# Four shifted taps in 32-column groups on TensorE: a depthwise convolution and its projection recast

## The chip, the cores and the metric

The kernel runs on one core of a Trainium2 chip. Its time is device microseconds from the first to the last instruction of one execution, median of several; lower is better. The engines are TensorE (PE, with its weight loads PEld), VectorE (DVE), ScalarE (ACT), GpSimd (POOL) and SyncE (SP, which here only issues DMAs).

## The reference

A decoder trunk of two layers on 512 tokens of 1024 channels, in float32. The change lies in the first half of the first layer, the Conformer convolution module; the rest is named only.

```python
def conformer_conv(x, w_pw1, b_pw1, w_dw, b_dw, ln_g, ln_b, w_pw2, b_pw2):
    a = jax.nn.glu(x @ w_pw1 + b_pw1, axis=-1)          # 1024 -> 2 x 1024, gated
    y = lax.conv_general_dilated(                        # causal, per channel, width 31
        a, w_dw[:, None, :].astype(a.dtype), window_strides=(1,),
        padding=((CONV_WIDTH - 1, 0),),
        dimension_numbers=('NWC', 'WIO', 'NWC'),
        feature_group_count=D_MODEL) + b_dw
    y = jax.nn.silu(layernorm(y, ln_g, ln_b))
    return y @ w_pw2 + b_pw2
...
h = h + conformer_conv(rmsnorm(h, norm_mix[0]), ...)
h = h + swiglu_ffn(rmsnorm(h, norm_ffn[0]), ...)
# second layer: attention over a window of 128 with a bias table, swiglu_ffn, final rmsnorm
```

## The kernel before

Channels lie on the 128 partitions, tokens along the free axis, so an activation is eight blocks (`ct` = 0 to 7) of 128 x 512. The order of instructions on each engine is made by a scheduler, from the order in which the program states them and from a model of their times; `issue_after` adds an edge to it. Most matmuls of the kernel take a weight and an activation that are each split into a rounded part and a rest (`float32r`), in three passes: `mm3`, lines 302 to 305. Weights come as chunks of 128 x 1024 in the order of `PLAN`. `get` (288) hands out a chunk and calls `advance` (236), which loads up to six chunks ahead (into four `raw` buffers, on SP's queue) and splits up to three ahead: a copy on ACT (247), a subtraction on DVE (248).

The convolution stage (599 to 822) goes so:

- Start (328 to 339, 748 to 768): x is loaded in eight rows of 256 KB on SP's queue, the first block's projection weights on ACT's. `Rms.add` squares on ACT and sums on POOL and DVE; the row sums and the norm's spread are two small matmul groups in the midst of the first projection.
- `Pw1` (625): the first projection in plain float32, 16 matmuls of 128 x 512 a block, two passes each in the trace, with weights `w1` that are loaded beside the plan. Block 0 uses x times the gain and applies the norm in its gate, the others use `xg` (766).
- `gate` (644): sigmoid of one half times the other half, into `apad`, a row of 30 zeros and 512 values.
- `Conv.taps` (684): of 31 taps a block, 19 (20, 13 in the last two) run on DVE as multiply-adds that gather in a PSUM bank (702, 704), 12 (11, 8) as products on ACT (694, 696) that POOL adds up (697) and joins (709). Ten taps of the last block are diagonal 128 x 128 matmuls (681).
- `shift_rows` (711) takes a mean of the first two blocks off all rows; `sums` (717) gathers column sums of y and its square with one-column matmuls (727); `scales` (732) makes mean and scale; `idle` (770) issues matmuls without use.
- `table` (612), at ct = 5: a small matmul and a scaling on ACT give the bias table, which one DMA on SP's queue writes out expanded to 3 MB of DRAM (`fd`, 617). Eight DMAs read it back after the stage (841).

Then the second projection `pw2` starts (824), PE at work without a break. In the attention, `values` makes matmuls of 128 x 64 weights into two halves of the output rows, all in a fixed order through `in_turn` (921), which the trace shows as line 923.

Of the kernel before, what the change touches and what calls it, by code (L numbers as in the profile page):

```python
# [17 lines left out]
P = 128  # L18
# [35 lines left out]
def chunk_plan():  # L54
    plan = []

# [19 lines left out]

    pw2()
# [22 lines left out]
CHUNKS = [("pw1", ct, half) for ct in range(KT) for half in range(2)]  # L100
CHUNKS += [c for c in dict.fromkeys(PLAN) if c[0] != "prod"]
# [29 lines left out]

def lay_params(w):
# [25 lines left out]
def hybrid_trunk(ctx: ExitStack, tc: tile.TileContext, xT, W, prm_in, wdw_in, sinks, relb, onehot, fin, out):  # L158
# [129 lines left out]
    def get(*key):  # L288
# [9 lines left out]
        n = {"kv": 4, "up": 4, "q": 4, "prod": 4}.get(key[0], 2)  # L298
        sh = dict(a=n)
        return tuple(w.rearrange("p (a b) -> p a b", **sh) for w in (hi, lo))  # L300

# [24 lines left out]
    w1, w1_in = {}, [None]  # L326

    def load_w1(ct, cuts=((0, 4), (4, 8)), queue=nc.sync):
        w1[ct] = quads.tile([P, KT, 2, P], F32, tag="quad", name=uid("w1"))
        for a, b in cuts:  # L330
            c = a % 4 * 256
            w1_in[0] = queue.dma_start(w1[ct][:, a:b].rearrange("p k w c -> p (k w c)"),
                            W[CHUNK_AT["pw1", ct, a // 4]][:, c:c + (b - a) * 256]).ins

    load_w1(0, ((0, 1), (1, 2), (2, 4), (4, 8)), nc.scalar)
    for i in range(KT):
        nc.sync.dma_start(hT[:, i, :], xT[i])
    nc.scalar.dma_start(wdw, wdw_in)
    load_w1(1)
    load_w1(2)  # L340
# [8 lines left out]
    make_identity(nc, ident)  # L349
    mhalf = cpool.tile([P, 4], F32, tag="mhalf", name="mhalf")  # L350
# [7 lines left out]
    class Rms:  # L358
        def __init__(self, bc):
            self.acc = {}  # L360
            self.bc = bc
            self.stage = 0

        def add(self, t, eng=nc.gpsimd):
            sq = temp()
            nc.scalar.square(sq, t)  # L366
# [4 lines left out]
        def step1(self):  # L371
# [5 lines left out]
            for n, (i, a) in enumerate(parts):  # L377
                mm = nc.tensor.matmul(st[:, i:i + 1], a[:, i * P:(i + 1) * P], ones_c, start=n == 0, stop=n == len(parts) - 1)
            self.summed = mm.ins
# [6 lines left out]
        def step2(self):  # L386
            self.step1()
            if self.stage != 2:
                self.stage = 2
                nc.scalar.copy(self.bc, spread(self.diag))  # L390
# [8 lines left out]
    def spread(diag):  # L399

        pb = bank()
        spread_ins[0] = nc.tensor.matmul(pb, ones_m, diag, start=True, stop=True).ins  # L402
        return pb

    spread_ins = [None]
# [193 lines left out]
    with conv_stage:  # L599
# [19 lines left out]
        a_pad = {}  # L619
        y = four_by()  # L620
        raw, xg = four_by(), four_by()
        st = None
        sums_done = [0]

        class Pw1:


            def __init__(self, ct, x, mid={}):
                self.ct = ct
                self.lin, self.gt = bank(), bank()  # L630
                order = [(k, w) for w in (1, 0) for k in range(KT)]
                if ct == 0:
                    order = [(k, w) for k in range(KT) for w in (1, 0)]
                hold = ExitStack()
                for k, w in order:
                    self.last = nc.tensor.matmul((self.lin, self.gt)[w], w1[ct][:, k, w, :], x[k],  # L636
                                                 start=k == 0, stop=k == KT - 1).ins
                    if ct == 0 and w == 0 and k in mid:
                        with tc.issue_after(self.last):
                            after = mid[k]()  # L640
                        hold.enter_context(tc.issue_after(after))
                hold.close()

            def gate(self, rs_bc=None):
                ct = self.ct
                a = a_pad[ct] = cv.tile([P, PAD + S], F32, tag="apad", name=uid("apad"), bufs=5)
                nc.gpsimd.memset(a[:, 0:PAD], 0.0)
                sig = temp()
                if rs_bc is None:
                    self.act = nc.scalar.activation(sig, self.gt, AF.Sigmoid, bias=col("b1", KT + ct)).ins  # L650
                else:
                    nc.vector.tensor_mul(sig, self.gt, rs_bc)
                    nc.scalar.activation(sig, sig, AF.Sigmoid, bias=col("b1", KT + ct))
                    nc.vector.tensor_mul(self.lin, self.lin, rs_bc)
                self.dve = nc.vector.scalar_tensor_tensor(a[:, PAD:], self.lin, col("b1", ct), sig,
                                                          op0=ALU.add, op1=ALU.mult).ins

        class Conv:


            shift = None

            def __init__(self, ct):
                self.ct = ct
                self.n_pool, self.n_pe = N_POOL[ct], N_PE[ct]
                self.nd = TAPS - self.n_pool - self.n_pe
                self.pe = None
# [4 lines left out]
            def diagonal_taps(self):  # L672
                if not self.n_pe:
                    return
                a = a_pad[self.ct]
                self.pe = bank()
                for n in range(self.n_pe):
                    j = TAPS - self.n_pe + n
                    dg = cv.tile([P, P], F32, tag="dg", name=uid("dg"), bufs=10)
                    nc.scalar.mul(dg, ident, self.tap(j))  # L680
                    mm = nc.tensor.matmul(self.pe, dg, a[:, j:j + S], start=n == 0, stop=n == self.n_pe - 1)  # L681
                self.last = mm.ins

            def taps(self):
                ct, nd, n_pool = self.ct, self.nd, self.n_pool
                a, yt, tap = a_pad[ct], y[ct], self.tap
                c = bank()
                acc, pi = None, 0
                for i in range(nd):
                    while pi * nd < n_pool * (i + 1):  # L690
                        j = nd + pi
                        pr = cv.tile([P, S], F32, tag="pr", name=uid("pr"), bufs=6)
                        if acc is None:
                            nc.scalar.activation(pr, a[:, j:j + S], AF.Identity, scale=tap(j), bias=col("bdw", ct))
                        else:
                            nc.scalar.mul(pr, a[:, j:j + S], tap(j))  # L696
                            nc.gpsimd.tensor_add(pr, acc, pr)  # L697
                        acc = pr
                        pi += 1
# [463 lines left out]
```

## Time and profile before

| | us |
|---|---|
| median of 3 runs | 1083.3 (1083.0 to 1083.49) |
| the profiled execution | 1084.53 |
| its span | 1082.7 |
| start of the second projection in it | 179.25 |
| DMA `fd`, issue to landing | 34.0 |

All times inside the kernel count from the start of the span. The page gives the busy time of each engine; the windows give it for one stretch; the chain of waits goes back from the last instruction to what released each; the groups (by line, operation and tile) give mean durations. A float32 matmul stands in the trace as two instructions of its line, one of `float32r` as one.

### The profile page before, as it was taken

The page shows a single profiled execution, that of the slowest core. Times are in us where ns is not written, and L with a number is a line of the kernel's source. Part 1 is how long each engine was busy: PE and PEld are TensorE (multiplying, and loading weights), DVE is VectorE, ACT ScalarE, POOL GpSimd, SP SyncE. Part 2 cuts the span into 40 slices and gives each one's busy share as a digit, 9 for nine tenths or more (in the row PEclk, how much of TensorE's full clock was granted, in tenths as well). Part 3 has the DMA queues.
Part 4 walks back from the last instruction along what each step waited for, and adds up shares of the span by engine and source line. Part 5 has one row for each costly group of instructions (what it writes and reads, how often), then busy time and mean ns, then how long its engine had stood idle before and what let it go on. Part 6 is the DMA issues. An engine that isn't in the chain of part 4 may idle for free.

```text
span 1082.7 us, 15381 instructions
## 1 busy us (share of the span) xinstructions
PE 1064.6 (98%) x6144; PEld 886.0 (82%) x6144; DVE 774.5 (72%) x1023; ACT 503.1 (46%) x770; POOL 214.9 (20%) x231
## 2 busy tenths in 40 slices
PE   8999989999999999999999999999999999999997
PEld 5445456888899899889988877788899988998996
DVE  3969997559977568658667677576979755776663
ACT  3666455335355245325535566454445531552353
POOL 2698890131000000000013244132100000000000
PEclk8999889999999999999999999999999999999999
DMA  9302542323334223512233211132423241243112
GB/s 354 120 1 78 60 57 78 106 91 102 112 117 136 78 79 98 162 42 90 83 113 97 78 45 54 40 109 85 156 79 98 97 156 59 79 135 117 40 59 78
DMA packets 33204, 103.47 MB, mean 96 GB/s; under 512 B 3659, under 2 KB 8684, under 8 KB 33132
## 3 DMA queue, kind: packets, MB, share of 16 engines
q1 hardware_dynamic: 31548, 100.21, 30.1%
q10 hardware_dynamic: 1584, 2.27, 0.6%
q8 instruction: 48, 0.79, 0.3%
q14 instruction: 24, 0.20, 0.1%
HBM read 97.23 MB, written 5.24 MB: 95 GB/s over the span
## 4 chain that ended last, share of the span: by engine, by line
PE 85%; POOL 5%; DVE 5%; issue 2%; ACT 2%; DMA 1%; POOLq 0%; SPq 0%; ACTq 0%
PE bank L303 22%; PE bank L304 22%; PE bank L305 22%; PE bank L923 12%; POOL pr L697 4%; DVE bank L704 2%; PE bank L1093 2%; PE bank L636 1%; PE bank L727 1%; PE bank L681 1%; DMA h<-in_xT_dram 1%; DVE quad L412 1%; PE bank L775 1%; PE bank L402 1%; ACT whi L247 1%
## 5 line engine op out<-in xcount | busy, mean ns | idle before, releaser
L304 PE MATMUL bank<-quad,whi 128*128 128x256 f32 (+1 forms) x1536 | 489.3, 320 | 0.9 <-DVE quad L412 0.9
L303 PE MATMUL bank<-quad,whi 128*128 128x256 f32 (+1 forms) x1536 | 484.2, 320 | 0.9 <-ACT tmp L559 0.6
L305 PE MATMUL bank<-quad,wlo 128*128 128x256 f32 (+1 forms) x1536 | 482.3, 319 | 0.0
L304 PEld LDWEIGHTS bank<-quad,whi 128*128 128x128 f32 x1536 | 292.5, 190 | 22.8 <-DVE quad L412 1.3
L303 PEld LDWEIGHTS bank<-quad,whi 128*128 128x128 f32 x1536 | 291.2, 190 | 23.3 <-ACT quad L415 1.1
L305 PEld LDWEIGHTS bank<-quad,wlo 128*128 128x128 f32 x1536 | 290.0, 190 | 20.8 <-issue 0.5
L247 ACT CAST whi<-raw 128x1024 fp32r<-128x1024 f32 x160 | 167.7, 1051 | 294.0 <-PE bank L304 195.2
L248 DVE TENSOR_TENSOR wlo<-raw,whi 128x1024 fp32r<-128x1024 f32 x160 | 202.3, 1267 | 106.6 <-ACT whi L247 99.0
L636 PE MATMUL bank<-quad,w 128*128 128x512 f32 x256 | 118.8, 625 | 0.5 <-DMA w<-in_W_dram 0.5
L697 POOL TENSOR_TENSOR pr<-pr,pr 128x512 f32<-128x512 f32 x83 | 108.0, 1312 | 25.4 <-ACT pr L696 21.5
L248 DVE TENSOR_TENSOR wlo<-blocks,whi 128x1024 fp32r<-128x1024 f32 x54 | 65.5, 1222 | 54.2 <-ACT whi L247 54.1
L636 PEld LDWEIGHTS bank<-quad,w 128*128 128x128 f32 x256 | 51.0, 202 | 64.7 <-issue 62.3
L247 ACT CAST whi<-blocks 128x1024 fp32r<-128x1024 f32 x54 | 56.6, 1048 | 86.8 <-PE bank L304 65.4
L704 DVE SCALAR_TENSOR_TENSOR bank<-apad,wdw,bank 128x512 f32<-128x512 f32 x135 | 94.3, 751 | 1.5
L923 PE MATMUL bank<-quad,whi 128*128 128x512 f32 x256 | 79.9, 393 | 0.0
L696 ACT ACTIVATE pr<-apad,wdw 128x512 f32<-128x512 f32 x83 | 58.5, 719 | 33.1 <-POOL pr L697 30.8
L368 POOL TENSOR_TENSOR tmp<-tmp,tmp 128x512 f32<-128x512 f32 x24 | 36.7, 1527 | 125.2 <-ACT tmp L366 69.3
L1104 POOL TENSOR_TENSOR rs<-ss,mhalf 128x1 f32<-128x1 f32 x4 | 2.2, 547 | 297.6 <-DVE ss L1102 297.6
L923 PEld LDWEIGHTS bank<-quad,whi 128*128 128x128 f32 x256 | 47.3, 188 | 9.9 <-issue 0.4
L966 POOL COPY sc<-sk 128x4 f32<-128x4 f32 x16 | 3.5, 252 | 257.0 <-DVE wlo L248 254.8
L923 PE MATMUL bank<-quad,wlo 128*128 128x512 f32 x128 | 49.9, 390 | 0.0
L990 POOL TENSOR_SCALAR sc<-sc,sm 128x256 f32<-128x256 f32 (+1 forms) x64 | 31.6, 514 | 66.1 <-DVE sm L988 66.0
(147 smaller groups left out, 1039.6 us busy)
## 6 DMA issues: line engine op xcount, KB each, us to landing
raw<-in_W_dram SPq DMA_DIRECT2D x124, 512.0 KB, 3.5
blocks<-in_W_dram SPq DMA_DIRECT2D x36, 512.0 KB, 4.6
w<-in_W_dram SPq DMA_DIRECT2D x14, 512.0 KB, 7.7
fd<-fs SPq DMA_DIRECT2D x1, 3072.0 KB, 34.0
h<-in_xT_dram SPq DMA_DIRECT2D x8, 256.0 KB, 5.7
bias<-fd SPq DMA_DIRECT2D x8, 256.0 KB, 4.8
out_dram<-hg SPq DMA_DIRECT2D x3, 256.0 KB, 2.0
out_dram<-hg ACTq DMA_DIRECT2D x3, 256.0 KB, 2.6
```

What stands on the lines that cost most here:

```text
L247: nc.scalar.copy(hi, r)
L248: lo_engine[0].tensor_sub(lo, r, f32(hi))
L303: nc.tensor.matmul(out, w[0], x[0], start=start, stop=False, **kw)
L304: nc.tensor.matmul(out, w[0], x[1], start=False, stop=False, **kw)
L305: nc.tensor.matmul(out, w[1], x[0], start=False, stop=stop, **kw)
L368: eng.tensor_add(sq, self.acc[eng], sq)
L636: self.last = nc.tensor.matmul((self.lin, self.gt)[w], w1[ct][:, k, w, :], x[k], start=k == 0, stop=k == KT - 1).ins
L696: nc.scalar.mul(pr, a[:, j:j + S], tap(j))
L697: nc.gpsimd.tensor_add(pr, acc, pr)
L704: nc.vector.scalar_tensor_tensor(yt if i == nd - 1 else c, src, tap(i), c if i else Conv.shift, op0=ALU.mult, op1=ALU.add)
L923: turn[0] = nc.tensor.matmul(*args, **kw).ins
L990: nc.gpsimd.tensor_scalar(sc[:, j, 1:1 + w], sc[:, j, 1:1 + w], sm[:, j:j + 1], 0.0, op0=ALU.mult, op1=ALU.add)
```

## The change

The first projection goes through the plan as 16 chunks and in three passes, from rows of x that are split with the gain; the norm is applied in each gate. Of each block's 31 taps the last 4 r run on PE in r rounds (3, 3, 3, 3, 3, 3, 4, 6). A round is four float32 matmuls, one for 32 channels each: the moving operand holds, on 4 x 32 partitions, those 32 channels' rows at four shifts, the weights are four diagonals of 32, and the output is 32 rows of the bank. To bring the rows into that form the padded block is written to DRAM and read back by four DMAs. DVE takes 10 (9, 7, 4) taps, ACT and POOL the rest: 9, 9, 9, 9, 9, 10, 8, 3. Matmuls of the stage go in one fixed order through `in_turn`. The rounds of block ct - 2 stand after the first half of block ct's projection. Column sums become 32-column matmuls over two blocks at a time. For the last three blocks DVE's taps don't wait for the rounds, which are added at the end. `table` stays at ct = 5 and is stated ahead of that block's gate.

```diff
-N_POOL = (12, 12, 12, 12, 12, 12, 11, 8)
-N_PE = (0, 0, 0, 0, 0, 0, 0, 10)
-N_AHEAD = (0, 16, 19, 19, 19, 19, 19, 19)
+ROUNDS = (3, 3, 3, 3, 3, 3, 4, 6)
+N_DVE = (10, 10, 10, 10, 10, 9, 7, 4)
...
+    W_CUTS = ((0, 0, 256), (0, 256, 512), (0, 512, 1024), (1, 0, 512), (1, 512, 1024))
+    for i, a, b in W_CUTS:
+        nc.scalar.dma_start(early[i][0][:, a:b], W[i][:, a:b])
...
+        for n, (i, a, b) in enumerate(W_CUTS):
+            for k in range(i * 4 + a // 256, i * 4 + b // 256):
+                split_scaled(x[k], h[k], col("mix0", k))
+            r, hi, lo = (t[:, a:b] for t in early[i])
+            nc.scalar.copy(hi, r)
+            begun = nc.vector.tensor_sub(lo, r, f32(hi)).ins
...
+        for k in range(KT):
+            rms0.add(h[k], (nc.gpsimd, nc.vector)[k // 4], own=k < 4)
...
+            def project(self, inside):
+                self.lin, self.gt = bank(), bank()
+                for half in range(2):
+                    whi, wlo = get("pw1", ct, half)
...
+                        mm3_in_turn((self.lin, self.gt)[w], (whi[:, k, sl], wlo[:, k, sl]), x[half * 4 + k],
+                                    half + k == 0, half == 1 and k == 3)
+                        inside(half, n)
...
+                n = S + 4 * (self.r - 1)
+                q = self.q = cv.tile([P, 4, S + 4 * (max(ROUNDS) - 1)], F32, tag="shifted", name=uid("shifted"))
+                row = PAD + S
+                ad = dpool.tile([P, row], F32, tag=uid("rows"), name=uid("rowsd"))
+                nc.sync.dma_start(ad, a)
+                for s in range(4):
+                    nc.sync.dma_start(q[s * 32:(s + 1) * 32, :, 0:n],
+                                      bass.AP(tensor=ad.tensor, offset=ad.offset + self.j0 + s,
+                                              ap=[[row, 32], [32 * row, 4], [1, n]]))
+                m = 4 * self.r
+                w = self.w = cv.tile([P, 4 * max(ROUNDS), 32], F32, tag="diag", name=uid("diag"))
...
+                    nc.vector.tensor_mul(w[:, 0:m], eye.unsqueeze(1).to_broadcast([P, m, 32]),
+                                         rnd[:, at:at + m].unsqueeze(2).to_broadcast([P, m, 32]))
+
+            def rounds(self):
+                self.c = bank()
+                for n in range(self.r):
+                    for g in range(4):
+                        in_turn(self.c[g * 32:(g + 1) * 32, :], self.w[:, g * self.r + n, :],
+                                self.q[:, g, 4 * n:4 * n + S], start=n == 0, stop=n == self.r - 1)
...
+        def sums(ct):
...
+            for n, t in enumerate(src):
+                in_turn(st[0][n * 32:(n + 1) * 32, :], ones32, t, start=ct == 0, stop=ct == KT - 2)
...
+        def inside(ct):
+            def at(half, n):
+                if ct == 1 and half == 0 and n == 1:
+                    rms0.step1()
+                if ct == 1 and half == 0 and n == 7:
+                    rms0.step2()
+                    convs[0].gate()
+                    convs[0].products()
+                if half == 0 and n == 7 and ct >= 2:
+                    convs[ct - 2].rounds()
+                if half == 1 and n == 7:
+                    if ct == 4:
+                        shift_rows()
+                    if ct == 5:
+                        table()
+                    if ct in (5, 6):
+                        sums(2 * ct - 10)
+            return at
+
+        for ct, c in enumerate(convs):
+            c.project(inside(ct))
+            if ct:
+                c.gate()
+                if ct >= 2:
+                    convs[ct - 2].taps()
+                c.products()
+            if ct == 3:
+                table_in()
+        convs[KT - 2].rounds()
+        for c in convs[KT - 2:]:
+            c.taps()
+        for c in convs[KT - 3:KT - 1]:
+            c.last()
+        sums(KT - 4)
+        convs[KT - 1].rounds()
+        convs[KT - 1].last()
+        idle(2)
+        sums(KT - 2)
+        idle(2)
         pm, prs = scales()
```

More of the change, by code (lines that the diff above doesn't have):

```diff
@@ L617, in table @@
             nc.sync.dma_start(fd.rearrange("q h k -> h q k"), fs.unsqueeze(1).to_broadcast([NH, P, 3 * P]))
-        a_pad = {}
+        x = Act(KT)
         y = four_by()
[L621 to L629, printed above, removed]
-                self.lin, self.gt = bank(), bank()
[L631 to L644, printed above, removed]
+        slots = four_by()
@@ L655, in gate @@
[L655 to L667, printed above, removed]
-            def tap(self, j):
-                return wdw[:, self.ct, j:j + 1]
[L672 to L682, printed above, removed]
+                nc.vector.tensor_mul(sig, self.gt, rs_bc)
```

277 lines of the change are left out of this document (138 added, 139 removed).

## Prediction, made before the changed kernel was run

> **What bounds the kernel now.** The change touches only the first layer's convolution stage, so the question is when that stage ends. The head of the page, then the windows of the stage, one row per part of it (columns: PE, PEld, DVE, ACT, POOL busy us with counts, granted clock, DMA share, GB/s):
>
> ```profile
> span 1082.7 us, 15381 instructions
> PE 1064.6 (98%) x6144; PEld 886.0 (82%) x6144; DVE 774.5 (72%) x1023; ACT 503.1 (46%) x770; POOL 214.9 (20%) x231
> 34.00:116.00 82.00, 79.04 (x208) 36.66 (x207) 67.99 (x91) 52.25 (x75) 74.53 (x60) 0.94 0.10 31
> 116.00:146.00 30.00, 26.34 (x74) 12.36 (x72) 29.93 (x47) 16.33 (x25) 25.76 (x22) 1.00 0.79 89
> 146.00:179.00 33.00, 32.95 (x108) 19.71 (x108) 27.12 (x44) 11.99 (x17) 18.55 (x15) 0.79 0.33 78
> ```
>
> TensorE is 98% busy over the whole span, but inside the stage PE, DVE and POOL are all close to full. The chain of waits, in order of time (start, length, what), says which of them ends last:
>
> ```profile
> 4.53 6.24 DMA h<-in_xT_dram
> ...
> 16.31 3.27 PE bank L378 x16
> ...
> 31.41 0.58 ACT rsbc L767
> ...
> 34.07 0.76 DVE apad L655
> 34.85 0.81 ACT pr L694
> ...
> 39.07 1.28 POOL pr L697
> 40.42 1.27 POOL pr L697
> ...
> 114.06 1.27 POOL quad L709
> 115.36 0.69 DVE quad L720
> 116.04 17.20 DVE bank L704 x27
> ...
> 146.03 6.71 PE bank L727 x32
> 152.75 10.67 PE bank L681 x20
> 163.42 3.43 PE bank L775 x8
> 166.85 3.47 PE bank L727 x32
> 170.32 1.84 PE bank L775 x2
> ...
> 179.25 1.20 PE bank L303 x4
> 180.45 0.23 PE bank L304
> ```
>
> POOL's additions of tap products carry it from 35 to 115 us, DVE's taps to 146, then PE: 64 column sums, the last block's diagonal matmuls and fillers. At 179.25 the second projection starts; from there PE runs without gaps, a matmul of L303 to L305 every 0.23 us. That tail I leave as it is: forecast = 1083.3 (median) + (new start of the second projection − 179.25). The profiled execution took 1084.53 us, its span 1082.7, so the differences are read in a run 1.2 us above the median.
>
> **The change, part by part.** Groups of instructions (count, then busy us and mean ns): of the page, and the x4 and x5 rows of 93 to 102 us, where four weight chunks are split; the x54 row is that subtraction later in the kernel, with POOL mostly at rest.
>
> ```profile
> L636 PE MATMUL bank<-quad,w 128*128 128x512 f32 x256 | 118.8, 625 | 0.5 <-DMA w<-in_W_dram 0.5
> L697 POOL TENSOR_TENSOR pr<-pr,pr 128x512 f32<-128x512 f32 x83 | 108.0, 1312 | 25.4 <-ACT pr L696 21.5
> L248 DVE TENSOR_TENSOR wlo<-raw,whi 128x1024 fp32r<-128x1024 f32 x4 | 8.0, 2052 | 0.0
> L248 DVE TENSOR_TENSOR wlo<-blocks,whi 128x1024 fp32r<-128x1024 f32 x54 | 65.5, 1222 | 54.2 <-ACT whi L247 54.1
> L697 POOL TENSOR_TENSOR pr<-pr,pr 128x512 f32<-128x512 f32 x5 | 9.9, 1980 | 0.3
> ```
>
> *Projection.* 128 fp32 matmuls are 256 passes of 3.43/8 = 0.43 us, 110 us. Three-pass they are 8 × 16 × 3 = 384 × 0.23 = 88 us: 22 us less PE. In exchange the 16 weight chunks must be split: 16 copies on ACT (L247) and 16 subtractions on DVE (L248).
>
> *DVE.* 147 taps (L702, L704) become 70; at 17.20/27 = 0.64 us that removes 49 us. Subtractions add 16 × 2.05 = 33 at the price they have beside a busy POOL (the x4 row), the eight products that build the round weights some 0.7 each, 5.6. Net about −10 us.
>
> *POOL.* 83 + 8 additions become 58 + 3 + 8 = 69, spaced 40.42 − 39.07 = 1.35 us: 93 us. But beside the four subtractions five additions took 9.9 us where 5 × 1.31 = 6.6 is normal, so each subtraction costs POOL 0.9: 13 us more. 106 us from the first product on; before, 91 × 1.35 = 123.
>
> *Start.* Today the first padded block stands at 34.07 + 0.76 = 34.8. After: the rows still come until about 12 us (the chain waits for one until 10.8), the split of the last takes some 1.5, and 15 matmuls of the first projection wait for it: it ends near 18. Two steps of the second projection later (1.4 us) stand the row sums (3.3 as now), then 18 matmuls (4.1), the spread (0.9), and copy and gate as now, 31.41 to 34.8: 3.4. That makes 31. The eight products xg fall away, but PE waited for the rows' sum, not for them alone.
>
> *Rounds.* 28 rounds of four matmuls, each 128x32 weights into its own 32 columns, fp32, so two passes: 224 passes. No 32-column matmul stands in the trace; the nearest is two 64-column groups, the attention's values (timeline of PE, then the source view):
>
> ```profile
> 628.15 1.51 PE L923 MATMUL bank<-prt,vq 128*64 128x256 f32 x12
> L923 PE MATMUL bank<-prt,vq x112: 379/379/430, 628.1 to 700.3; 128*64 128x256 f32 x112
> ```
>
> Twelve passes, the last 0.38 long, so the starts spread over 1.13 us. A pass of 256 columns alone takes half of 0.43, 0.215; 1.13 is five such steps, so the twelve started in six pairs: two groups run side by side. I carry that to four: a round costs 2 × 0.43 = 0.86 us, all 28 of them 24 us. Bounds: four passes side by side 0.86; one after another 8 × 0.43 = 3.43, 96 us. I take the lower end because it is what the row shows for two.
>
> [...]
>
> PE per block is then 48 × 0.23 + 3 × 0.86 = 13.6 us, POOL 10 × 1.35 + 2 × 0.9 = 15.3, DVE 10 × 0.64 + gate 3 × 0.7 + subtractions 2 × 2.05 + weights 0.7 = 13.3. All three are full again, no longer POOL and DVE alone.
>
> *Sums and tail.* The single-column sums, of which the chain holds the last 64 passes with 6.71 + 3.47 us, become four calls of 4 column-group matmuls, 0.86 each. The loads of w1, all issued at the start, become chunks in the weight stream, less traffic early and none of it on the path. ACT gives up 25 of 91 products for the 16 copies; at 52 of 82 us it has room. The 10.67 us of diagonal matmuls become six rounds, 5.2 us. From the last sum to the second projection it was 179.25 − 170.32 = 8.9; the new way (copy of the sums, four small matmuls, the same power and spreads) I put at 8.9 too.
>
> *The queue.* The change adds per block a copy of the padded rows to DRAM (277 KB) and four reads back (266 KB each), 40 DMAs, all on SP's queue. The expanded bias table `fd` is issued there too, after the sixth projection (ct=5), where it was; today nothing of the stage stands behind it:
>
> ```profile
> fd<-fs SPq DMA_DIRECT2D x1, 3072.0 KB, 34.0
> 7.80 2.93 SPq L332 DMA_DIRECT2D w<-in_W_dram  x4
> 10.78 0.42 SPq L607 DMA_DIRECT2D sk<-in_sinks_dram  x1
> 11.25 0.43 SPq L608 DMA_DIRECT2D lhs<-in_relb_dram  x1
> sk<-in_sinks_dram SPq DMA_DIRECT2D x1, 8.0 KB, 7.5
> lhs<-in_relb_dram SPq DMA_DIRECT2D x1, 2.0 KB, 7.2
> prm<-in_prm_dram ACTq DMA_DIRECT2D x1, 48.0 KB, 3.0
> DMA to landing us min/median/max: 2.9/5.7/6.2
> ```
>
> `fd` takes 34 us to land. And the queue is served in order: 8 KB (sk) behind four 512 KB loads took 7.5 us, while 48 KB with nothing ahead took 3.0. So a block's rows issued behind `fd` land after it.
>
> [...]
>
> How long write and reads take alone the trace doesn't show. Below: the 2.9 us of a 256 KB load of rows (last row, the minimum over h), then 1.06 MB at the 415 GB/s of the stage's start, 2.6 plus the same latency, 7 together; above: `fd`, from 16 partitions, got 97 GB/s, so 2.9 + 11 + 2. Each read fills 32 partitions; I take 9.4, nearer the loads.
>
> ```profile
> GB/s 0 0 134 267 377 376 367 254 363 415 401 361 372 411 393 429 421 421 410 421 421 277 132 346 414 421 431 410 415 421 421 410 404 410 415 399 415 415 404 410
> GB/s 0 0 0 0 0 0 10 104 97 97 98 96 97 97 98 96 96 96 96 97 98 98 98 108 96 101 96 97 97 98 97 95 82 0 0 0 0 0 0 0
> ```
>
> (GB/s in 40 slices, of 0 to 30 us and of 110 to 160 us.)
>
> **The forecast: a block's copies wait behind the table.** PE ends the first projection at 18, the second with row sums and norm at 18 + 11 + 3.3 + 0.9 = 33. Block 0's reads land at 31 + 9.4, when PE has stood 2 us before its rounds, in the middle of the third. Then 13.6 a block: the sixth ends at 35 + 4 × 13.6 + 1.7 (shift rows) = 91. Table matmul and scaling follow, `fd` is issued at 93 and landed at 127. Block 5's rows are ready at 94, behind it; with write and reads the rest takes 7.5 (its start is hidden), 134.5. Its rounds stand in PE's fixed order in the middle of the eighth projection, which PE reaches at 91 + 1.7 + 13.6 + 0.9 + 5.5 = 112.7. PE waits 22 us, and so does everything in turn behind: half a projection, the last gate, the rounds of blocks 6 and 7. From 134.5: three rounds 2.6 and the clock's loss 2.1 (after the 3.7 us that PE lacks in 116 to 146 the next window's clock is 0.79, and 20 passes took 10.67 instead of 8.6), 24 × 0.23 = 5.5, gate 2.5, write and reads 9.4, six rounds 5.2, last addition, square and sums 2.6, tail 8.9: 173.3, that is −6.0 us. **1077 us.** If `fd` goes between blocks 5 and 6, only the rounds of 6 and 7 wait: landed 131, reads 144.5, rounds 149.7, start 161: 1065. If POOL's 15.3 a block sets the pace to the sixth, `fd` goes 7 us later: 1084; reads at the upper bound both times add 6. Range of this case 1064 to 1087.
>
> **Rivals.**
> 1. *Nothing waits behind the table* (it gets in early, or the reads pass it). PE passes the eighth projection at 112.7 + 2.6 + 5.5 = 121, gate 123.5, write and reads 133, six rounds 138; POOL from 32 with 106 us ends at 138 too. 138 + 2.6 + 8.9 = 149.5: −30 us, 1053 (1050 to 1062). For it: one DMA that is ready early can be issued early, as sk was, at 10.78 us. Against: its matmul needs a PSUM bank at the sixth projection.
> 2. *The column groups don't run four at a time.* Slower than before. Two at a time cost 0.86 more a round, 25 rounds on the path: 1077 + 21 = 1098; one pass at a time 2.57 more, with the sums 70: 1147. It decides from 6.0/25 = 0.24 us, that is from a round of 1.1 us on. For it: four streams and 32-column loads are shown nowhere. Against: the pairs above.
> 3. *The change doesn't give the engines relief*: splits starve PE, because each subtraction takes 2.05 us and waits for ACT's copy. 16 × (2.05 − 1.22) us uncovered is 13 us: 1077 + 13 = 1090.
>
> **How the numbers follow.** Forecast case 0.55, rival 1 0.27, rival 2 0.12, rival 3 0.06. Predicted 1077. The range leaves out rival 2, rival 3 and the lowest end of rival 1: 1052 to 1087. A difference under 0.2% (2.2 us) can't be told from none. Within the forecast case `fd`'s place gives faster 0.40, same 0.09, slower 0.06. With rival 1 faster 0.67, and of rivals 2 and 3, should they meet rival 1's start, 0.03 faster and 0.01 same: faster 0.70, same 0.10, slower 0.20.
>
> **What would show it.** A round of four takes 0.86 us on PE; the second projection's start moves from 179 to about 173; PE idles some 20 us before the rounds of a block, with that block's reads named as releaser and landing just after `fd`; the first padded block at 31. Wrong if the rounds take over 1.2 us, if no read lands late, or if DVE's subtractions end PE's waits.

## The result, and the profile after

The changed kernel takes 1107.2 us (median of 4 runs, 1106.7 to 1108.0) where the kernel before takes 1083.2 on the same chip: ratio 1.022 (1.021 to 1.024). It is 24 us slower; 1077 had been forecast. The head of its page and the windows of the stage (start:end, length, then busy us and count of PE, PEld, DVE, ACT and POOL, granted clock, DMA share, GB/s), to set against those of before:

```profile
span 1105.0 us, 15906 instructions
PE 1048.8 (95%) x6388; PEld 895.9 (81%) x6388; DVE 760.3 (69%) x983; ACT 501.2 (45%) x760; POOL 203.6 (18%) x213
34.00:116.00 82.00, 78.99 (x395) 52.95 (x393) 65.21 (x76) 51.28 (x72) 72.26 (x51) 0.98 0.63 149
116.00:146.00 30.00, 7.64 (x33) 4.85 (x32) 16.79 (x20) 12.92 (x18) 23.15 (x18) 0.68 0.87 127
146.00:179.00 33.00, 18.54 (x92) 7.41 (x96) 16.57 (x23) 5.07 (x7) 6.74 (x5) 0.71 0.66 161
```

Up to 116 us all is as full as before. From 116 to 146 PE works 7.6 of 30 us, where it worked 26.3. The chain of waits (start, length, what) says on what:

```profile
37.27 2.27 DMA rowsd<-apad
...
41.75 5.14 DMA shifted<-rowsd
46.99 4.26 PE bank L319 x24
...
117.91 26.60 DMA rowsd<-apad
...
145.90 5.78 DMA shifted<-rowsd
151.81 11.18 PE bank L319 x48
...
166.89 4.20 DMA rowsd<-apad
...
172.46 6.07 DMA shifted<-rowsd
178.62 15.81 PE bank L319 x80
```

The copy of block 0's rows to DRAM takes 2.3 us; that of block 5 takes 26.6, since it stands behind the bias table. SP's timeline (start, time that the issue took) and one row each of the waits and of the transfers:

```profile
107.75 0.30 SPq L644 DMA_DIRECT2D fd<-fs  x1
108.89 8.93 SPq L245 DMA_DIRECT2D raw<-in_W_dram  x1
117.91 4.43 SPq L714 DMA_DIRECT2D rowsd<-apad  x1
122.43 4.51 SPq L245 DMA_DIRECT2D raw<-in_W_dram  x1
144.59 1.74 SPq L716 DMA_DIRECT2D shifted<-rowsd  x4
```

```profile
PE bank L319 <- DMA shifted<-rowsd: 36.5, 3, 28.2
fd<-fs SPq DMA_DIRECT2D x1, 3072.0 KB, 34.8
```

`fd` is issued at 107.75 and lands 34.8 us later, at 142.5; block 5's copy lands at 144.5, its reads at 151.7, and PE has stood 28.2 us. What stands behind the rounds of block 5 follows one after the other (half a projection, the last gate, copy, reads, rounds, sums), and the second projection starts at 199.1 instead of 179.25. These 19.8 us, with 2.5 us of short waits and half speed behind that start (passes 0.43 us apart from 202.2 to 204.3 us, 0.23 after), are the 22.3 us between the two spans.

### The profile page after: what moved, and what is told of

The parts are those of the page before. It is cut to its first block, busy times and chain, and to the rows that moved or that the text cites. A ratio compares the mean times of both kernels' runs of the same rounds, so it can differ in the third digit from the quotient of the medians.

```text
span 1105.0 us, 15906 instructions
## 1 busy us (share of the span) xinstructions
PE 1048.8 (95%) x6388; PEld 895.9 (81%) x6388; DVE 760.3 (69%) x983; ACT 501.2 (45%) x760; POOL 203.6 (18%) x213
## 4 chain that ended last, share of the span: by engine, by line
PE 84%; DMA 5%; POOL 4%; DVE 3%; issue 2%; ACT 1%; SPq 0%; POOLq 0%; ACTq 0%
PE bank L328 22%; PE bank L327 22%; PE bank L329 22%; PE bank L319 16%; POOL quad L745 3%; DMA rowsd<-apad 3%; DMA shifted<-rowsd 2%; PE bank L1123 1%; DMA h<-in_xT_dram 1%; DVE quad L439 1%; POOL quad L757 0%; DVE wlo L261 0%; ACT quad L743 0%; SPq L716 0%; DVE bank L753 0%
## 5 line engine op out<-in xcount | busy, mean ns | idle before, releaser
L260 ACT CAST whi<-raw 128x1024 fp32r<-128x1024 f32 x174 | 182.3, 1050 | 309.8 <-PE bank L328 191.9
L328 PEld LDWEIGHTS bank<-quad,whi 128*128 128x128 f32 x1536 | 292.9, 191 | 24.1 <-DVE quad L443 1.3
L327 PEld LDWEIGHTS bank<-quad,whi 128*128 128x128 f32 x1536 | 291.7, 191 | 24.4 <-ACT quad L442 2.1
L329 PEld LDWEIGHTS bank<-quad,wlo 128*128 128x128 f32 x1536 | 290.4, 191 | 20.8 <-issue 0.5
L261 DVE TENSOR_TENSOR wlo<-raw,whi 128x1024 fp32r<-128x1024 f32 x174 | 221.4, 1274 | 124.6 <-ACT whi L260 112.2
L319 PE MATMUL bank<-quad,whi 128*128 128x512 f32 x512 | 163.8, 401 | 4.9 <-ACT whi L667 4.9
L319 PEld LDWEIGHTS bank<-quad,whi 128*128 128x128 f32 x512 | 96.5, 192 | 34.4 <-ACT whi L667 5.2
L319 PE MATMUL bank<-quad,wlo 128*128 128x512 f32 x256 | 101.2, 395 | 0.6 <-DVE wlo L668 0.6
L745 POOL TENSOR_TENSOR quad<-quad 128x512 f32<-128x512 f32 x58 | 83.1, 1436 | 14.9 <-ACT quad L743 11.6
L319 PE MATMUL bank<-shifted,diag 128*32 128x512 f32 x224 | 31.0, 699 | 36.5 <-DMA shifted<-rowsd 36.5
L319 PEld LDWEIGHTS bank<-quad,wlo 128*128 128x128 f32 x256 | 48.7, 190 | 11.8 <-DVE wlo L668 1.1
L743 ACT ACTIVATE quad<-apad,wdw 128x512 f32<-128x512 f32 x58 | 40.6, 719 | 23.3 <-POOL quad L745 23.2
L439 DVE SCALAR_TENSOR_TENSOR quad<-h,prm,quad 128x512 fp32r<-128x512 f32 x40 | 43.0, 1104 | 8.0 <-ACT quad L438 7.5
## 6 DMA issues: line engine op xcount, KB each, us to landing
fd<-fs SPq DMA_DIRECT2D x1, 3072.0 KB, 34.8
```

What stands on the lines that cost most here:

```text
L260: nc.scalar.copy(hi, r)
L261: lo_engine[0].tensor_sub(lo, r, f32(hi))
L319: turn[0] = nc.tensor.matmul(*args, **kw).ins
L327: nc.tensor.matmul(out, w[0], x[0], start=start, stop=False, **kw)
L328: nc.tensor.matmul(out, w[0], x[1], start=False, stop=False, **kw)
L329: nc.tensor.matmul(out, w[1], x[0], start=False, stop=stop, **kw)
```

## The experiments

Every kernel was timed against the kernel before on its own chip (e1 to e4 on one; e5 to e8 and e13 on a second; e9 to e12 on a third). Executions of one kernel spread over 1 to 9 us there (before: 1080.7 to 1086.4 in 28 runs), so differences under 2 us between kernels are not read. All start from the changed kernel; "profiled" is the time of the profiled execution, which can lie 3 us beside the median, and "pw2" the start of the second projection in it.

| kernel | median us | ratio to before, interval | profiled | pw2 |
|---|---|---|---|---|
| e1 table's write behind the last reads | 1084.7 | 1.001 (1.000 to 1.002) | 1085.5 | 179.1 |
| e2 table's write on ACT's queue | 1102.6 | 1.018 (1.016 to 1.020) | 1102.4 | 196.1 |
| e3 table at the third block | 1107.2 | 1.023 (1.020 to 1.025) | 1110.3 | 202.3 |
| e4 = e1 with a plain first projection | 1087.1 | 1.003 (1.002 to 1.004) | 1087.7 | 180.7 |
| e5 write from 128 partitions | 1084.2 | 1.000 (0.998 to 1.001) | 1084.5 | 178.2 |
| e6 = e1 with the last gate first on DVE | 1089.2 | 1.004 (1.002 to 1.006) | 1086.2 | 179.9 |
| e7 = e1 with 18 matmuls at the start | 1084.6 | 1.001 (1.000 to 1.003) | 1084.5 | 176.8 |
| e8 = e1, last block by diagonals | 1087.6 | 1.003 (1.002 to 1.004) | 1085.1 | 179.0 |
| e9 = e5 with e6's and e7's edits, rounds before sums | 1084.5 | 1.002 (1.000 to 1.003) | 1083.6 | 177.4 |
| e10 = e5 without the rounds of five blocks | 1105.9 | 1.021 (1.020 to 1.023) | 1106.4 | 198.5 |
| e11 = e9, fillers moved | 1078.7 | 0.996 (0.994 to 0.997) | 1080.9 | 172.8 |
| e12 = e9, fillers dropped | 1079.1 | 0.997 (0.996 to 0.999) | 1079.1 | 172.7 |
| e13 = e5, fillers dropped | 1082.6 | 0.999 (0.998 to 1.000) | 1080.4 | 174.2 |

### Where the table's write stands: e1, e2, e3

e1 states `table()` behind the loop and holds its DMA until the last block's reads are issued; e2 puts the same DMA on ACT's queue; e3 makes the table three blocks earlier (and loads its inputs two earlier).

```diff
 e1
-                    if ct == 5:
-                        table()
...
+            with tc.issue_after(read[0]):
+                nc.sync.dma_start(fd.rearrange("q h k -> h q k"), fs.unsqueeze(1).to_broadcast([NH, P, 3 * P]))
 e2
-            nc.sync.dma_start(fd.rearrange("q h k -> h q k"), fs.unsqueeze(1).to_broadcast([NH, P, 3 * P]))
+            nc.scalar.dma_start(fd.rearrange("q h k -> h q k"), fs.unsqueeze(1).to_broadcast([NH, P, 3 * P]))
 e3
-                    if ct == 5:
+                    if ct == 2:
...
-            if ct == 3:
+            if ct == 1:
                 table_in()
```

> The bias table's matmul, scaling and expanded write are stated behind the last block's four reads, nothing else changes. Theory (the reads of block 5 wait in SP's queue behind the 3 MB write): the 28.2 us that PE waits before that block's rounds vanish with no new wait of more than 4 us, the second projection starts at 165 to 171 instead of 199.1, the time is 1107 - 31 = 1076, 1072 to 1080. Rival (the reads, or POOL's additions, are late by themselves and the write only stands beside them): the wait stays or comes back before another block's rounds, less than 8 us are won, 1099 or more.

> The write of the table is issued at the same place, but on ACT's queue. Theory (order within one queue): the reads pass it, only slowed by sharing the 16 engines packet by packet; a row's packet (some 90 ns) alternates with one of the table (218 ns), so copy and reads of block 5 take some 18 us instead of 11, against 14 us of slack: PE waits 4 to 8 us, 1083, 1078 to 1090. Rival (the DMA engines themselves are taken for 34 us, whatever the queue): the wait stays near 28 us, 1102 to 1110.

> The table stands in the third projection (ct=2) instead of the sixth. Theory (any block's reads have the same slack, so the write costs the same wherever reads stand behind it): PE waits 22 to 30 us before the rounds of block 2, and the time is that of the changed kernel within 6 us, 1101 to 1113. Rival (the place is what costs: early, seven chunks of weights and the gates ahead cover it): 1090 or less.

With nothing behind it (e1) the write costs nothing: 22.5 us come back and the wait of 28.2 is gone, though the time is 1084.7 and not 1076, and waits of 6.2 and 8.3 us stand before the rounds of blocks 6 and 7, where none over 4 had been expected. Three blocks earlier (e3) it costs the same as at the sixth: PE waits 25.8 us before the rounds of block 2. Another queue (e2) gives back under 5 us, and PE still waits 24.6. e2's chain of waits:

```profile
109.26 21.44 DMA rowsd<-apad
...
131.16 4.52 SPq L716
135.73 4.51 SPq L716
140.28 7.48 DMA shifted<-rowsd
147.90 10.73 PE bank L319 x48
```

On its own queue the copy no longer waits for the whole write, but it takes 21.4 us instead of 2.3, and two of the four reads behind it cost SP 4.5 us each to issue. So it was not the order of one queue alone: the write slows what runs beside it on the other queue too. From 108 to 142 us 2060 packets of ACT's queue and 548 of SP's moved, and the copy landed at 130.7, while the write, with 35.3 us to land, was still under way: both queues moved data side by side, as at the changed kernel's start (158 packets of SP's queue and 147 of ACT's from 3 to 4 us). But copy and reads took 38.5 us from the copy's issue to the last landing, not the 18 for which the expectation had a row's packet and one of the table take turns.

### Why the write is slow: e5

The table lies on 16 partitions. e5 makes eight copies of each head's row by 128 weight columns in the same matmul, so that the source lies on 128; place and queue stay.

```diff
-        lhs = cv.tile([NBUCKET + 1, NH], F32, tag="lhs", name="lhs", bufs=1)
+        lhs = cv.tile([NBUCKET + 1, 8, NH], F32, tag="lhs", name="lhs", bufs=1)
-        fs = cv.tile([NH, 3 * P], F32, tag="fs", name="fs", bufs=1)
+        fs = cv.tile([P, 3 * P], F32, tag="fs", name="fs", bufs=1)
-            nc.sync.dma_start(fd.rearrange("q h k -> h q k"), fs.unsqueeze(1).to_broadcast([NH, P, 3 * P]))
+            nc.sync.dma_start(fd.rearrange("(j r) h k -> (r h) j k", r=8), fs.unsqueeze(1).to_broadcast([P, 16, 3 * P]))
```

> The changed kernel with the bias table's write left at the sixth block, but its source spread over 128 partitions (each head's row in eight copies, by 128 weight columns in the table's matmul) where it lay on 16. In the changed kernel a packet of 1536 bytes of this write took 218 ns, where packets elsewhere go down to 62 ns, and the write took 34.8 us to land. Theory (the engines are occupied by slow packets from 16 partitions, and everything behind the write or beside it waits that long): with packets near 62 ns the write lands some 10 us after its issue, PE's wait before the rounds of block 5 falls from 28 us to 3 to 5, and the time is 1083 (1080 to 1088). Rival (3 MB in pieces of 1536 bytes cost this on the DRAM side whatever the source): the write still takes some 35 us and the time stays at 1107 (1104 to 1110).

The write lands in 10.8 us, PE's longest wait for reads falls from 28.2 to 5.1, and the time is that of before. Transfers, throughput from 105 to 125 us in 40 slices, and the wait, of e5; then the throughput of the changed kernel from 108 to 142:

```profile
fd<-fs SPq DMA_DIRECT2D x1, 3072.0 KB, 10.8
GB/s 0 0 0 0 0 0 33 0 3 273 378 372 369 372 378 381 362 384 369 378 372 375 378 366 289 215 200 236 311 324 365 415 409 410 221 45 83 316 295 208
PE bank L319 <- DMA shifted<-rowsd: 12.7, 3, 5.1
```

```profile
GB/s 34 101 96 101 94 98 98 101 96 99 98 98 99 96 98 96 98 99 98 94 101 98 98 96 99 98 98 99 96 99 96 101 94 96 101 94 99 87 120 285
```

375 GB/s against 98, from the same bytes in the same pieces; the traces have a packet of 1536 bytes at 67 ns (median) in e5 and at 222 in the changed kernel. That refutes the rival: pieces of this size are not slow in themselves. With its source on 16 partitions the write had 0.26 of the throughput that it has from 128. With the partitions e5 also changes the order in which the pieces go out; no run tells the two apart.

### What the two parts bring: e4 and e10

e4 undoes the three-pass projection (plain float32 from unsplit chunks), e10 the rounds of blocks 0 to 4 (DVE takes their twelve taps).

```diff
 e4
-                        mm3_in_turn((self.lin, self.gt)[w], (whi[:, k, sl], wlo[:, k, sl]), x[half * 4 + k],
+                        in_turn((self.lin, self.gt)[w], whi[:, k, sl], x[half * 4 + k],
 e10
-ROUNDS = (3, 3, 3, 3, 3, 3, 4, 6)
-N_DVE = (10, 10, 10, 10, 10, 9, 7, 4)
+ROUNDS = (0, 0, 0, 0, 0, 3, 4, 6)
+N_DVE = (22, 22, 22, 22, 22, 9, 7, 4)
```

> As e1_table_late, and the first projection in plain float32 from unsplit chunks, as before the change: rounds alone. Theory (with the table out of the way PE sets the pace of a block: 48 x 0.23 + 2.7 = 13.8 us, in plain float32 16 x 0.86 + 2.7 = 16.5): eight blocks cost 21 us more, the start some 5 less, 1076 + 16 = 1092, 1086 to 1097. Rival (splits and their collision with POOL set the pace): same as e1_table_late or faster, 1078 or less.

> The changed kernel with the table's write from 128 partitions (1084.2), without the rounds of blocks 0 to 4: their twelve taps each run on DVE as multiply-adds (22 instead of 10), and their copies to DRAM, reads and round weights fall away. It measures what the rounds bring by themselves. Theory (a round gives four taps for 0.86 us of PE, and DVE, as full as POOL, gets 12 x 0.66 = 7.9 us a block more and loses the weights' 0.7): DVE needs 20.5 us a block instead of 13.3, against the 15 a block that these blocks took, so five blocks take 25 to 30 us longer, 1110 (1104 to 1118). Rival (POOL and the waits around the gates set the pace and DVE has air): less than 15 us longer, under 1099.

e4 is 2.4 us above e1, between 16 more (the theory) and none (the rival); that 1087.1 lies inside the theory's range is luck, since e1 itself came out 8.7 above what that range was built on. The three passes free PE, but e4's window shows PE at 82 of 82 us with DVE at 45.5 (65.8 in e1's), so the splits load DVE where PE is relieved; that the one pays for the other is argued, not shown. e10 costs some 22 us against e5, 4.4 a block; DVE, at 65.3 in e5's window, is at 78.7. The rounds are the part that pays: 1105.9 lies in the range, though 22 is less than the 25 to 30 of the theory. Window 34 to 116 of e4, then of e10:

```profile
34.00:116.00 82.00, 82.00 (x278) 32.64 (x280) 45.53 (x62) 42.23 (x62) 65.88 (x55) 1.00 0.58 152
```

```profile
34.00:116.00 82.00, 61.76 (x255) 47.39 (x254) 78.73 (x100) 47.57 (x67) 63.71 (x47) 0.85 0.22 71
```

### Why no gain is left without the stall: e6 to e9, e11 to e13

In e1 the last projection leaves PE at 132.3, but the last padded block stands only at 144.6 and its rounds begin at 157.0 (chain of waits of e1):

```profile
144.66 4.28 DMA rowsd<-apad
...
150.32 6.59 DMA shifted<-rowsd
157.00 17.40 PE bank L319 x80
```

Three single edits of e1 attack the late start, the late gate and the round trip through DRAM.

```diff
 e6
+                    with tc.issue_after(c.gated) if ct == KT - 1 else nullcontext():
-                    convs[ct - 2].taps()
+                        convs[ct - 2].taps()
 e7
-N_WARM = 7
+N_WARM = 18
 e8 (last block; no copy, no reads)
+                    for j in range(self.j0, TAPS):
+                        in_turn(self.c, self.dg[j - self.j0], self.a[:, j:j + S], start=j == self.j0, stop=j == TAPS - 1)
```

> The kernel with the table's write behind the last block's reads (1084.7), and block 5's taps on DVE held until the last block's gate is done. There the last projection left PE at 132.4, but the last padded block stood only at 144.6, since DVE did nine taps of block 5, two weight subtractions of 2.3 us and the round weights ahead of or between the three steps of the gate. Theory (what is exposed at the end is the chain last gate, copy, reads, rounds, and DVE's order starts it 8 us late): padded block at 136 to 137, rounds of the last block some 8 us earlier, time 1077 (1074 to 1080). Rival (DVE's total work sets the end, and the held taps come late instead): the last rounds start earlier, but y of block 5 or 6 is late and the sums wait for it, 1082 to 1086.

> The kernel with the table's write behind the last block's reads (1084.7), with 18 instead of 7 matmuls of ones ahead of the first projection, so that PE has work until 9.1 us where it stood still from 4.4 to 9.3 or 10.6. Theory (after that pause PE runs passes 0.427 us apart until 17.5, then 0.227, and this makes the first padded block late): passes 0.227 apart from the start, the first padded block 3 to 5 us earlier, and as the chain runs through it, the time 3 to 4.5 less: 1081 (1079.5 to 1082). Rival (DVE's splits of rows and chunks set the first projection, PE would only wait between passes): first padded block within 1 us of where it was, time 1084 to 1085.

> The kernel with the table's write behind the last reads (1084.7), in which the last block's 24 taps on PE are 24 matmuls with diagonal 128x128 weights straight from the padded block instead of six rounds, so that its copy to DRAM and its four reads fall away; ACT makes 24 diagonals more, and the table's write stands behind block 6's reads. In the kernel it changes, the padded block stood at 144.6, the rounds began at 157.0 and their sum was added at 165.3. Theory (this round trip of 12.4 us lies open at the end): the matmuls begin at 144.8 and take 24 x 0.43 = 10.3 us (12.8 at the price of 0.53 each that ten of them had in the kernel before), the sum is added at 156 to 158, 8 to 9 us earlier: 1076 (1074 to 1079). Rival (the other engines end the stage then: POOL's last addition came at 153.2, or ACT's diagonals hold PE up): no more than 3 us, 1081 to 1085.

None wins. In e6 the padded block does come at 136.9, but PE's fixed order has the sums of blocks 4 and 5 ahead of the last rounds, and the held taps finish their y at 157: its rival, though the time is 3 us above that rival's range. In e7 the first padded block stands at 36.9, where e1 has it at 38.7. But in the nine kernels with seven matmuls at the start and three passes it stands anywhere from 36.7 to 38.7, in the four with 18 from 36.9 to 37.6: about 0.6 us on average, not 3 to 5, and e7's time is its rival's. The passes run at full speed at once (0.23 us apart), and then wait for the row splits on DVE. PE's timeline of the changed kernel, then of e7 (start, length, a matmul, count, in brackets the idle time before it and its releaser):

```profile
9.26 1.43 PE L319 MATMUL bank<-quad,whi 128*128 128x512 f32 x2 [4.89 <-ACT whi L667]
...
15.75 1.05 PE L319 MATMUL bank<-quad,whi 128*128 128x512 f32 x2
16.61 0.63 PE L319 MATMUL bank<-quad,wlo 128*128 128x512 f32 x1
...
20.00 0.62 PE L319 MATMUL bank<-quad,whi 128*128 128x512 f32 x2
20.46 0.39 PE L319 MATMUL bank<-quad,wlo 128*128 128x512 f32 x1
```

```profile
18.18 0.61 PE L319 MATMUL bank<-quad,whi 128*128 128x512 f32 x2
18.63 0.39 PE L319 MATMUL bank<-quad,wlo 128*128 128x512 f32 x1
18.86 0.39 PE L319 MATMUL bank<-quad,whi 128*128 128x512 f32 x1
19.84 0.50 PE L319 MATMUL bank<-quad,whi 128*128 128x512 f32 x1 [0.59 <-DVE quad L439]
```

For e8 I had priced a diagonal tap at 0.43 us; that is one pass, and it takes two. 24 taps took as long as the round trip and the rounds together (e8's PE timeline, where the row's 48 are passes):

```profile
144.51 20.87 PE L319 MATMUL bank<-apad,dg 128*128 128x512 f32 x48
```

e6 and e8 were timed 3 to 5 us above e1 although their pw2 is that of e1 within 0.9 us. But their profiled executions, with 1086.2 and 1085.1, lie 3.0 and 2.5 below their medians. The sixth padded block stands at 108.0 and 107.7 us in them and at 109.8 in e1's; from there to pw2 e1 takes 69.2 us, e6 2.7 and e8 2.1 more. In the eleven kernels that do much the same up to that block (all but e3, e4 and e10) it stands anywhere from 107.3 to 110.4, so pw2 of two kernels is to be read together with it. What moves it is not known.

e9 puts the wide write, e6's and e7's edits and a changed order on PE together.

```diff
-        sums(KT - 4)
         convs[KT - 1].rounds()
+        sums(KT - 4)
```

> The changed kernel with four edits together: the table's write from 128 partitions (at the sixth block, as in the change), block 5's taps on DVE held until the last gate is done, the last block's rounds stated ahead of the sums of blocks 4 and 5 in PE's fixed order, and 18 matmuls of ones at the start. With the held taps alone the last padded block had come at 136.9 instead of 144.6, but PE's order put the sums of blocks 4 and 5 first, whose y DVE and POOL finished at 157, so that the rounds began as late as before. Theory (write, order of DVE and order of PE are the three waits left at the end, and only together do they pay): rounds of the last block begin at 147 to 149, DVE's last addition ends at 155 to 158, the second projection starts at 170 to 174 (179.25 in the kernel before), and the time is 6 to 9 less than the kernel before, 1075 to 1078. Rival (the stage's length is set by the work of DVE and POOL, whose last y comes near 157 in each of these kernels, and the rest of the tail is longer than it looks): second projection at 177 or later, time within 3 of the kernel before.

The rounds begin at 148.9 as expected, and y is complete at 159.2, a little behind the 155 to 158 expected; yet the second projection starts at 177.4 and the time is 1084.5, the numbers of the rival. PE's timeline of e9 shows what eats the gain:

```profile
148.88 6.75 PE L319 MATMUL bank<-shifted,diag 128*32 128x512 f32 x48 [8.06 <-DVE quad L754]
155.44 1.04 PE L319 MATMUL bank<-quad,ones_m 128*32 128x512 f32 x4
159.22 9.20 PE L319 MATMUL bank<-quad,ones_m 128*32 128x512 f32 x20 [2.75 <-DVE quad L762]
168.26 0.95 PE L319 MATMUL bank<-sel,tmp 128*128 128x2 f32 x8
```

Between 159.2 and 168.3 stand twelve passes of sums and eight of `idle`, the fillers; PE comes out of a wait of 2.75 us at half speed (granted clock 0.50 from 159 to 163), and the first four passes of fillers take 0.85 to 1.0 us each, in front of the last sums. The rounds, too, were released by DVE's last tap of block 5 (L754), not by their reads: so much of the rival holds. e11 drops two fillers, keeps one behind the sums and puts eleven into the waits; e12 drops the four; e13 drops them from e5.

```diff
-        idle(2)
         sums(KT - 2)
-        idle(2)
```

> The kernel of the four edits, in which y was complete at 159.2 but the second projection began only at 177.4. There PE stood still from 140.8 to 148.9 and from 156.5 to 159.2; after both waits its passes were 0.66 to 0.85 us apart where 0.43 is normal, and two filler matmuls (0.85 us a pass, four passes) stood between the last square and the last sums. Edit: the two fillers between the sums go, the two behind them become one, eight fillers stand behind block 6's rounds and three behind the last rounds, in the waits. Theory (the gain on the other engines was given back on PE: half speed after each wait, and fillers on the path): rounds of the last block in 5.2 us instead of 6.8, sums at full speed right behind the last square, second projection at 171 to 173.5, time 1078 to 1081 where the four edits gave 1084.5. Rival (what ends the stage is elsewhere): second projection at 176 or later, 1083 to 1085.

> The same four edits with the fillers around the last sums dropped and none put into the waits. It tells the fillers' own time from the half speed after a wait. Theory: the four passes of 0.85 us ahead of the last sums and the four of 0.43 behind them go, but the rounds still take 6.8 and all sums run at half speed (0.86 more), so the second projection starts 1 to 2.5 us later than with fillers in the waits: 173 to 175, 1080 to 1082. If the half speed after a wait costs nothing here, both kernels start it within 0.5 us of each other.

> The changed kernel with the table's write from 128 partitions and without the four fillers around the last sums, the order of DVE and PE and the start as they were (1084.2 with the fillers, second projection at 178.24). Theory (the fillers only cost where the gate has already come early): here the last rounds end at 164.2, the first two fillers at 166.2, the square of the last block at 165.9, so they hide the addition and the square and take 0.3 us, and the second pair takes 1.2 at most: second projection at 176.8 to 178, time 1083 to 1084.2. Rival (the fillers alone are what the kernel with all edits won): second projection at 172.5 to 174, time 1078 to 1080.

e12's timeline at the same place:

```profile
159.15 3.61 PE L319 MATMUL bank<-quad,ones_m 128*32 128x512 f32 x12 [2.75 <-DVE quad L762]
163.44 1.05 PE L319 MATMUL bank<-sel,tmp 128*128 128x2 f32 x8 [0.67 <-ACT tmp L798]
```

y is complete at the same moment, `sel` starts 4.8 us earlier, the second projection 4.7, and the time falls by 5.4. e11 and e12 are the first that are faster than the kernel before, by 0.4% (0.3 to 0.6) and 0.3% (0.1 to 0.4). Fillers in the waits add nothing beside their absence on the path: both start pw2 within 0.1 us. e11's numbers came out as forecast, its reason did not: its rounds took 7.1 us, not 5.2, for the eight fillers ended 2.5 us ahead of them, and in the rounds, from 152 to 154, the granted clock was 0.50. What full speed there would bring was not measured. PE's timeline of e11:

```profile
140.52 7.13 PE L319 MATMUL bank<-quad,ones_m 128*128 128x512 f32 x16
150.13 7.05 PE L319 MATMUL bank<-shifted,diag 128*32 128x512 f32 x48 [2.48 <-DVE quad L754]
```

Dropped alone (e13) the fillers bring 1.6 us, too little to be told from none. Of the 4.0 us by which pw2 comes earlier there (178.2 to 174.2), 2.4 stand already at the sixth padded block, ahead of any edit. e12 lies 3.5 below e13 by its median, but on another chip and with executions from 1077.3 to 1083.3; from the sixth padded block to pw2 it is 0.8 us shorter. How much the other edits bring beside the fillers is therefore not settled.

## Why the prediction was wrong

**The mechanism was right.** PE stood before the rounds of block 5 with their reads named as releaser, just after `fd` had landed, and e1 and e5, which take away the write's place or its length, take away the loss. The reason given, the order of one queue, is only part of it: in SP's queue the copy issued at 117.91 landed 2.0 us after `fd`, at 144.5, but on the other queue (e2) it still took 21.4 us. Rival 1 (nothing waits) is refuted.

**The rounds: right.** 0.86 us each: three take 2.78 with the last pass's end where PE runs at full speed. Four groups of 32 columns run side by side (rival 2, for which two at a time would make 4 × 0.43 = 1.72 us a round, is refuted):

```profile
62.42 2.78 PE L319 MATMUL bank<-shifted,diag 128*32 128x512 f32 x24
```

**The step that failed: "`fd` is issued at 93 and landed at 127".** It was issued at 107.75 and landed at 142.5. Of the 14.8 us, 6.6 came before block 0's rounds, which began at 47.0 instead of 40.4: the first padded block stood at 37.2, not 31, and its copy and reads took 0.4 more. The term at fault is the first projection, which ended at 24.8 and not near 18: the sum had the last row split by about 13.5, and DVE finished it at 21.2. That PE had no work until 9.3 and then ran at half speed until 17 (passes 0.427 us apart) matters less: with more matmuls ahead the block comes some 0.6 us earlier (e7), without the splits it stands at 34.8 (e4). 2.3 were lost over the next blocks (the sixth projection ended 52.9 after block 0's rounds, not 50.6). 5.9 lay where the prediction had put almost nothing: the scaling of the table ran on ACT only at 107.26, though its matmul began at 100.24, because it stands in ACT's order behind products that wait for POOL (first and last rows of ACT's timeline there):

```profile
100.76 0.63 ACT L784 ACTIVATE quad<-quad 128x512 f32<-128x512 f32 x1 [1.82 <-POOL quad L757]
...
107.26 0.46 ACT L642 ACTIVATE fs<-bank 16x384 f32<-16x384 f32 x1
```

The prediction had a later `fd` only as a variant (POOL sets the pace, 7 us, 1084), and there through PE's pace, not through ACT's order.

**The remaining terms, all on one side.** `fd` 34.8 for 34; copy and reads behind it 9.3 for 7.5; from block 5's rounds to pw2 47.3 for 38.8, namely rounds 0.6 more, half projection 0.3, last gate 3.9 for 2.5, copy and reads 11.7 for 9.4, last rounds 6.6 for 5.2, addition, squares and sums 4.7 for 2.6, tail 0.3. With the 14.8 that is 25.8 us: pw2 at 199.1, not 173.3. The rest of the 30 us between 1077 and 1107.2 is the 2.5 behind that start, and 1.5 because the profiled execution before lay 1.2 above its median and that of the changed kernel 0.3 below. The range reached up to 1087 because each of these was varied by itself, as if the others would hold.

**The price without the stall was as wrong.** Rival 1 put pw2 at 149.5; e1 and e5, without the stall, have it at 179 and 178. The eighth projection ended at 132.3 instead of 121 (start and pace), the last gate took 12 us instead of 2.5 (DVE's order, as e6 shows), and copy and reads 12.4 instead of 9.5 (11.4 in e5, where `fd` had landed long before). So the change had not a large gain that one wait took away; without that wait it is level with the kernel before.

**The projection's 22 us of PE.** They were taken for relief; e4 shows 2.4 us. Rival 3 is half true: splits did hold PE up at the start (first padded block at 34.8 without them, 38.7 in e1), but undoing them is no faster.

What stays open: what moves the sixth padded block by up to 3 us between executions, and why copy and reads take 11.4 to 12.4 us at the end of the stage and 9.8 at block 0.

## What to carry to other kernels

Before a chain of small DMAs is put on a queue, look for the long transfer in the same stage, and look at its source: here a write from 16 partitions ran at 98 GB/s against 375 from 128 and held up copies and reads on either queue that was tried, and spreading its source cost one wider matmul. A producer's place in the order of its own engine (here a 0.46 us scaling behind 6 us of products) belongs in the sum as much as the queue of its DMA. Where an order is written out by hand, fillers and sums in it are tied to the old waits: an earlier gate won nothing by itself (e6), nor with the orders on DVE and PE (e9), and 0.3 to 0.4% against the kernel before once the fillers had followed (e11, e12).

## What the runs showed of the hardware

The three issues behind `fd` on SP took 8.9, 4.4 and 4.5 us, where the median of their lines is 0.33; with the write on the other queue (e2) it was 4.2 for the copy and 4.5 for two reads. After a wait of 2.75 us PE went on at half speed in e9, at a granted clock of 0.50 from 159 to 163 us, where the mean from 150 to 157 had been 0.88. In the changed kernel's start the passes are 0.427 us apart too, after a wait of 4.9 us, but the granted clock there is given as 1.00 (0.50 in the same window of e5): the spacing of the passes is the surer sign. The window 9 to 17 of the changed kernel, then 159 to 163 of e9:

```profile
9.00:17.00 8.00, 7.11 (x15) 5.04 (x16) 8.00 (x10) 8.00 (x16) 3.32 (x3) 1.00 0.74 278
```

```profile
159.00:163.00 4.00, 3.77 (x6) 1.12 (x7) 0.17 (x1) 0.63 (x1) 0.00 (x0) 0.50 0.00 0
```
